# Softmax bias, rope queries and a weight fetch in another order, the last half tile cut 384 + 128: one layer of a hybrid diffusion trunk on one Trainium2 core

## The chip, the core and the metric

The kernel runs on one core of one Trainium2 chip. Its five engines are named as in the profile: PE is TensorE (matmul), DVE is VectorE, ACT is ScalarE, POOL is GpSimd and SP is SyncE, which here only issues DMAs. The metric is the device time of one execution in microseconds (us). Before the change the median of three runs is 616.72 us (616.5 to 617.53).

## The reference

One layer of a hybrid trunk for 1024 latent tokens and 128 context tokens, width 1024, float32. Each token goes through an RMSNorm with modulation and one input projection to 2496 columns, which feeds a gated MLP (group A) and a latent attention with 4 heads (group B). Latent tokens read 1024 latent keys, whose rope part is rotated, and 256 cached context keys, whose rope part isn't. Both groups' outputs go through one output projection, are gated, added to the residual, and a last RMSNorm scales each row.

```python
h = _rmsnorm(x, norm_g) * (1 + scale) + shift
u, v, g_a, c_q, c_kv, k_rope, g_b = _split_in(h @ w_in)
a_out = _chunk_mlp(u, v, w_s, b_s, g_v) * jax.nn.silu(g_a)
q = (_rmsnorm(c_q, q_norm_g) @ w_uq).reshape(B, L, MLA_HEADS, QK_NOPE + QK_ROPE)
...
attn = _block_attention(qn, (qr_rot, qr), ((kn, kr_rot, vv), (kn_c, kr_c, v_c)))   # softmax over 1024 + 256 keys
y = jnp.concatenate([a_out, attn * jax.nn.silu(g_b)], axis=-1) @ w_o
return _rmsnorm(x + gate * y, final_g)
```

## The kernel before

**Tiles and stages.** A row tile is 128 tokens: tiles 0 to 7 are the latent tokens, tile 8 is the context. Each operand of a product is held as a high and a low float32r part, and a product is three matmuls (high by high, high by low, low by high). The stages follow each other on PE: the input projection and the gated MLP (to about 300 us of the span), the transposes of queries and keys (to 318), the attention (318 to 530), and the output projection with the last norms (530 to the end).

**The attention stream.** A head is a query tile t with a head number h. `score_steps(t, h)` writes the logits of the 1024 latent keys to a PSUM tile `s1` in two halves (`lat`, lines 1515 to 1519), and those of the 256 context keys to a half of `s2` (`con`). Softmax has four steps in `softmax`: `start` (DVE maximum of the latent logits, into `m`, L1481), `shift` (DVE maximum of the context logits, L1484, and the bias `nb`, by one operation at L1489 or by two at L1486 and L1487), `exps` (ACT exponentials of the context and then the latent logits into `e`, L1495) and `divide` (DVE sum and reciprocal `rs`, L1499 and L1500, then POOL scales `e`, L1501). Two heads are a pair. `value_steps(t, pr)` then takes a pair's 1280 columns in five steps: PE transposes four 128x128 blocks of `e` into a PSUM tile `pT` (L1562), ACT copies its high part into `ph` (L1566), DVE subtracts to get the low part `pl` (L112, a helper that all such subtractions share), and PE multiplies both with the values into `o` (L1586 to L1588). After the fifth step ACT copies `o` to `os`, and PE projects it into `at` (L1605), which lies in a buffer of the same pool as `pT`; DVE multiplies it into `mixB` (L1607). So every pair of heads is one period of the stream, with one `at`.

**What sets the order.** All engines run what the program writes, in that order. A hand-kept clock `now` advances by an assumed cost with every PE step, and `later(dt, fn)` puts `fn` into the program once that clock has gone on by `dt`. So `dt` is no wait: it sets only what stands ahead of what in the queue of an engine.

**Beside the attention.** A list `units` holds 16 jobs that form sums of blocks of the output weights `w_o` for a Strassen-like output projection: SP loads `traw`, POOL forms differences, ACT copies high parts `thi`, DVE subtracts the low parts in `traw`, and SP writes all to `tdram`. They run beside query tiles 1 to 5. Later `t_pieces(m, ...)` fetches sum number m back with DMAs that POOL issues (L1919). `his` and `los` are lists of jobs for spare moments of POOL and DVE.

**Rope queries.** `q_rope_T(t)` transposes a tile's rotary queries into `qrT`, copies their high parts on ACT (L1339) and subtracts the low parts on DVE (L1347).

**Output projection and the end.** `Plan` takes steps with an engine, a cost, a priority and what they need, and writes them in the order of a greedy schedule. 28 products run with blocks of sums; five PSUM banks "w" are shared between them. `load_gate` (L2053) fetches the gate rows, with which DVE multiplies each finished product (L2194 for one of the first). `norm` ends each row tile: ACT squares, a root, three to four small DVE steps, then `y6` as one DVE operation over 128x1024 (L2120) and `y7` as two ACT operations (L2128) with DMAs from ACT's queue, after POOL multiplied with the final gain `fg` (L2132). Tile 8's right half is done early and kept; `finish_left` does its left half last: `left` writes two PSUM tiles of 256 columns (24 matmuls each, L1952 to L1954), DVE multiplies with the gate row (`zm`, L2278) and adds the residual (`za`, L2279), ACT squares, DVE forms the mean `zv` (L2286), ACT the root (L2287), four DVE steps the reciprocal root `rlast`, and DVE and ACT scale the left (L2296) and the kept right half (L2300), each with its own store.

Of the kernel before, what the change touches and what calls it, by code (L numbers as in the profile page):

```python
# [13 lines left out]
AF = mybir.ActivationFunctionType  # L14
# [6 lines left out]
NS = 8  # L21
# [73 lines left out]
def tile_hymba_step(ctx: ExitStack, tc: tile.TileContext, I, O):  # L95
# [1225 lines left out]
    def q_rope_T(t):  # L1321
# [14 lines left out]
        def part(par):  # L1336
            own = slice(64 * par, 64 * par + 64)
            oth = slice(64 - 64 * par, 128 - 64 * par)
            later(0.0, lambda: S.copy(d5[own, 2 - n :, :, par, sl], src[own]))  # L1339
# [9 lines left out]
        later(0.1 if t == 7 else 0.6, lambda: part(0))  # L1349
        later(0.15 if t == 7 else 1.2, lambda: part(1))  # L1350
# [120 lines left out]
    def softmax(t, h, lat_, con_):  # L1471
# [11 lines left out]
        def shift():  # L1483
            V.tensor_reduce(m[:, 1:2], con_, axis=AX.X, op=ALU.max)  # L1484
            if units or (t, h) == (NS - 1, 3):
                V.tensor_reduce(nb, m, axis=AX.X, op=ALU.max)  # L1486
                V.tensor_scalar(nb, nb, nscl[:, t : t + 1], None, op0=ALU.mult)  # L1487
            else:
                V.scalar_tensor_tensor(nb, m[:, 0:1], m[:, 1:2], nscl[:, t : t + 1], op0=ALU.max, op1=ALU.mult)  # L1489
            later(0.6, exps)  # L1490
            later(1.3, lambda: spare_lo(1))
# [29 lines left out]
    def score_steps(t, h):  # L1521
# [266 lines left out]
    with tc.manual_schedule(engines=engines):  # L1788
# [311 lines left out]
    def norm(g, prio):  # L2100
# [6 lines left out]
        on_v(f"n{t}v", lambda: V.tensor_scalar(fv, fs, 1.0 / 1024.0, EPS, op0=ALU.mult, op1=ALU.add), prev, prio, 0.16)  # L2107
        prev = [f"n{t}r", f"n{t}v"]
        for i, fn in enumerate((
            lambda: V.reciprocal(r(), ft),  # L2110
            lambda: V.scalar_tensor_tensor(fw, fv, -0.5, r(), op0=ALU.mult, op1=ALU.mult),
            lambda: V.tensor_tensor(fw, fw, r(), op=ALU.mult),
            lambda: V.scalar_tensor_tensor(r(), fw, 1.5, r(), op0=ALU.add, op1=ALU.mult),
# [3 lines left out]
        for i, u in enumerate(g):  # L2117
# [5 lines left out]
            if u < 7:  # L2123
                on_v(f"y{u}", scale, [*prev, "fg"], prio, 1.8 if u < 6 else 1.3)
                continue

            def scale_half(c, i=i, u=u):
                S.activation(xr[u][:, c], xr[u][:, c], AF.Copy, scale=ssq[g][:, i : i + 1])  # L2128
                nc.scalar.dma_start(O["y"][u][:, c], xr[u][:, c])

            for j, c in enumerate((R, L)):
                on_g(f"fg7.{j}", lambda c=c, u=u: G.tensor_tensor(xr[u][:, c], xr[u][:, c], fg[:, c], op=ALU.mult), [f"sq7.{j}", "fg"], 3)  # L2132
                on_s(f"y7.{j}", lambda c=c: scale_half(c), [*prev, f"fg7.{j}"], 2, 0.72)
# [125 lines left out]
    def finish_left():  # L2259
        v, v0, root, u = (small(1) for _ in range(4))  # L2260
# [6 lines left out]
        H = slice(0, 256)  # L2267

        def left(j, c):
# [3 lines left out]
            out_terms(8, cell[j][:, H], c.start, c.stop, range(8))  # L2273

        for j, c in enumerate((slice(0, 256), slice(256, 512))):
            o = lambda j=j: cell[j][:, H]
            on_t(f"pz{j}", 2.9, lambda j=j, c=c: left(j, c), [], takes=("w",) if j else ("w", "w"))
            on_v(f"zm{j}", lambda o=o, c=c: V.tensor_tensor(o(), o(), g()[:, c], op=ALU.mult), [f"pz{j}", "own0"], 0.5, 0.42)  # L2278
            on_v(f"za{j}", lambda o=o, c=c: V.tensor_tensor(o(), o(), x()[:, c], op=ALU.add), [f"zm{j}"], 0.5, 0.42)  # L2279
        square(8, 0, lambda: cell["junk"][:, 0:256], L, ["za0"], 0.5, lambda: cell[0][:, H])  # L2280
# [3 lines left out]
            "zq", lambda: S.activation(cell["junk"][:, 256:512], cell[1][:, H], AF.Square, accum_out=ssq[(8,)][:, 2:3]), ["za1"], 0.4, 0.6  # L2284
        )
        on_v("zv", lambda: V.scalar_tensor_tensor(v, ssq[(8,)][:, 2:3], 1.0 / 1024.0, v0, op0=ALU.mult, op1=ALU.add), ["zq", "zv1"], 0.4, 0.2)  # L2286
        on_s("zr", lambda: S.activation(root, v, AF.Sqrt), ["zv"], 0.3, 0.25)  # L2287
# [3 lines left out]
        on_v("zr3", lambda: V.scalar_tensor_tensor(r, u, 1.5, r, op0=ALU.add, op1=ALU.mult), ["zr2"], 0.3, 0.18)  # L2291
# [11 lines left out]
        on_v("zo0", out0, ["zr3", "fg"], 0.3, 0.7)  # L2303
# [110 lines left out]
```

## Time and profile before

| | before |
|---|---|
| median of the runs | 616.72 us |
| the profiled execution's own time | 616.81 us |
| its span on the core | 615.0 us |
| mean granted TensorE clock | 0.993 |
| PE busy | 597.7 us, 3671 instructions |
| DVE busy | 426.2 us, 932 instructions |
| ACT busy | 330.0 us, 765 instructions |
| POOL busy | 204.7 us, 243 instructions |
| bytes moved by DMA | 67.33 MB |

The span is the profiled part of an execution; 1.8 us lie around it. A row of the timeline reads: start, duration, engine, line, operation, output and inputs by the program's names (numbers of buffers left out), shape and count, and in brackets the idle time of the engine just ahead of it with what ended that time. "PE L1562" is line 1562 of the kernel before. Starts of neighbours overlap by up to some 0.1 us, since an engine begins one instruction while the one ahead of it drains.

### The profile page before, as it was taken

The page shows a single profiled execution, that of the slowest core. Times are in us where ns is not written, and L with a number is a line of the kernel's source. Part 1 is how long each engine was busy: PE and PEld are TensorE (multiplying, and loading weights), DVE is VectorE, ACT ScalarE, POOL GpSimd, SP SyncE. Part 2 cuts the span into 40 slices and gives each one's busy share as a digit, 9 for nine tenths or more (in the row PEclk, how much of TensorE's full clock was granted, in tenths as well). Part 3 has the DMA queues.
Part 4 walks back from the last instruction along what each step waited for, and adds up shares of the span by engine and source line. Part 5 has one row for each costly group of instructions (what it writes and reads, how often), then busy time and mean ns, then how long its engine had stood idle before and what let it go on. Part 6 is the DMA issues. An engine that isn't in the chain of part 4 may idle for free.

```text
span 615.0 us, 10220 instructions
## 1 busy us (share of the span) xinstructions
PE 597.7 (97%) x3671; PEld 540.0 (88%) x3671; DVE 426.2 (69%) x932; ACT 330.0 (54%) x765; POOL 204.7 (33%) x243
## 2 busy tenths in 40 slices
PE   7999999999999999999999999999999999999994
PEld 6678889999989999999998899899999988788884
DVE  3674458997746368476678677777778765478885
ACT  5656764345433345455576566566655552457543
POOL 2452112000000000443273344544444456259831
PEclk9999999999999999999999999999999999999998
DMA  8993010000351124100001033443241015961452
GB/s 316 376 371 108 0 35 2 35 0 4 135 207 70 68 84 144 41 1 1 1 14 63 1 120 129 130 138 121 95 153 46 1 70 185 388 248 44 150 174 113
DMA packets 30627, 67.33 MB, mean 109 GB/s; under 512 B 3296, under 2 KB 17392, under 8 KB 29424
## 3 DMA queue, kind: packets, MB, share of 16 engines
q1 hardware_dynamic: 27360, 55.41, 25.7%
q0 software_dynamic: 2064, 8.39, 4.0%
q10 hardware_dynamic: 1152, 2.88, 1.2%
q8 instruction: 29, 0.48, 0.3%
q14 instruction: 22, 0.18, 0.1%
HBM read 53.45 MB, written 13.21 MB: 108 GB/s over the span
## 4 chain that ended last, share of the span: by engine, by line
PE 81%; DVE 10%; ACT 4%; issue 2%; DMA 1%; SPq 0%; ACTq 0%; DVEq 0%
PE p L954 10%; PE tp L752 8%; PE tp L976 5%; PE pT L1562 4%; DVE pl L112 3%; PE zacc L1390 2%; PE zacc L1389 2%; PE zacc L1391 2%; PE S L1923 2%; DVE m L1481 2%; PE S L1924 2%; PE S L1925 2%; ACT e L1495 2%; PE s L1518 2%; PE s L1516 2%
## 5 line engine op out<-in xcount | busy, mean ns | idle before, releaser
L1501 POOL TENSOR_SCALAR e<-e,rs 128x1280 f32<-128x1280 f32 x32 | 47.1, 1472 | 101.8 <-ACT ph L1566 69.8
L1495 ACT ACTIVATE e<-s,nb,scl 128x256 f32<-128x256 f32 x64 | 56.1, 881 | 41.7 <-DVE nb L1487 21.5
L112 DVE TENSOR_TENSOR pl<-pT,ph 128x512 fp32r<-128x512 f32 x81 | 55.4, 687 | 32.5 <-ACT ph L1566 30.7
L1566 ACT CAST ph<-pT 128x512 fp32r<-128x512 f32 x80 | 46.4, 588 | 33.4 <-PE pT L1562 31.8
L1237 POOL TENSOR_TENSOR kr<-z,rope 128x64 f32<-128x64 f32 x8 | 2.6, 325 | 172.0 <-ACT z L1246 172.0
L752 PE MATMUL tp<-area,w 128*128 128x384 f32 x288 | 52.5, 338 | 0.0
L1562 PE MATMUL pT<-ident,e 128*128 128x128 f32 x320 | 48.4, 274 | 2.7 <-DVE pl L112 2.0
L752 PEld LDWEIGHTS tp<-area,w 128*128 128x128 f32 x288 | 50.4, 188 | 0.4
L1586 PE MATMUL o<-ph,vh 128*128 128x256 f32 x160 | 47.7, 298 | 0.0
L1588 PE MATMUL o<-ph,vl 128*128 128x256 f32 x160 | 45.0, 281 | 0.0
L1587 PE MATMUL o<-pl,vh 128*128 128x256 f32 x160 | 44.9, 281 | 0.0
L1562 PEld LDWEIGHTS pT<-ident,e 128*128 128x128 f32 x320 | 37.0, 140 | 7.5 <-PE at L1605 2.5
L1481 DVE TENSOR_REDUCE m<-s 128x1 f32<-128x1024 f32 x32 | 38.9, 1216 | 1.5 <-PE s L1519 1.5
L1515 PE MATMUL s<-kch,area 128*128 128x512 f32 (+2 forms) x100 | 39.1, 391 | 0.0
L1516 PE MATMUL s<-kcl,area 128*128 128x512 f32 (+2 forms) x100 | 35.3, 353 | 0.0
L1518 PE MATMUL s<-krh,area 128*128 128x512 f32 (+2 forms) x100 | 35.3, 353 | 0.0
L1519 PE MATMUL s<-krl,area 128*128 128x512 f32 (+2 forms) x100 | 35.1, 351 | 0.0
L1517 PE MATMUL s<-kch,area 128*128 128x512 f32 (+2 forms) x100 | 35.1, 351 | 0.0
L976 PE MATMUL tp<-area,w 128*128 128x384 f32 x192 | 35.0, 337 | 0.0
L976 PEld LDWEIGHTS tp<-area,w 128*128 128x128 f32 x192 | 33.6, 188 | 0.4 <-issue 0.4
L1587 PEld LDWEIGHTS o<-pl,vh 128*128 128x128 f32 x160 | 30.2, 189 | 1.4
L1586 PEld LDWEIGHTS o<-ph,vh 128*128 128x128 f32 x160 | 30.1, 188 | 1.4
(665 smaller groups left out, 1718.6 us busy)
## 6 DMA issues: line engine op xcount, KB each, us to landing
ada<-in_ada_ss SPq DMA_DIRECT2D x16, 512.0 KB, 8.7
w2r<-in_w_t SPq DMA_DIRECT2D x12, 512.0 KB, 4.3
x<-in_x SPq DMA_DIRECT2D x9, 512.0 KB, 8.2
adag<-in_ada_g SPq DMA_DIRECT2D x4, 1024.0 KB, 4.9
traw<-in_w_o SPq DMA_DIRECT2D x16, 256.0 KB, 3.4
tdram<-thi SPq DMA_DIRECT2D x32, 128.0 KB, 1.8
tdram<-traw SPq DMA_DIRECT2D x32, 128.0 KB, 1.8
wor<-in_w_o SPq DMA_DIRECT2D x8, 512.0 KB, 3.6
```

The costliest lines, as they stand in the source:

```text
L112: V.tensor_tensor(lo, src, f32(hi), op=ALU.subtract)
L752: T.matmul(tps[i, g][:, :GW], w_[i][:, k, :], x_[k, g], start=k == 0 and j == 0, stop=k == NK - 1 and j == 2)
L954: T.matmul(banks[key], a_, b_, start=k == 0 and m == 0, stop=k == 3 and m == len(passes) - 1)
L976: T.matmul(tps[c, 2][:, :GW], w_[c][:, k, :], x_[k, 2], start=k == 0 and m == 0, stop=k == NK - 1 and m == 2)
L1481: V.tensor_reduce(m[:, 0:1], lat_, axis=AX.X, op=ALU.max)
L1495: S.activation(e[:, sl], src, AF.Exp, bias=nb, scale=scl[:, t : t + 1], accum_out=su[:, i : i + 1])
L1501: G.tensor_scalar(e, e, rs, 0.0, op0=ALU.mult, op1=ALU.add)
L1516: T.matmul(ps, qh_, kcl[:, sl], start=False, stop=False)
L1518: T.matmul(ps, qr_, krh[:, sl], start=False, stop=False)
L1562: T.transpose(ps[:, w : w + P], es[t, h][:, c * P : (c + 1) * P], ident)
L1586: T.matmul(o, vh[:, kt, :], ph[:, sl], start=c == 0, stop=False)
L1587: T.matmul(o, vh[:, kt, :], pl[:, sl], start=False, stop=False)
```

## The change

Seven edits, in the order of the program. (1) The bias `nb` is formed by two DVE operations also for query tiles 0 and 1. (2) `shift` is put into the queue 0.95 after the context logits where it was 0.7, while `units` has jobs and for tile 1. (3) The rope queries of tile 7: the ACT copies are written 8.2 later on the clock of the program, where it was 0.1, and the DVE subtractions follow at 1.4 and 2.5 behind them. (4) The fetch of the third sum of weights, two DMAs of POOL's queue, is put into the program 0.6 after the fourth `plain` step instead of at the end of the list `his`. (5) In `norm` the mean is multiplied by −0.5 when it is formed; tile 7 (a norm of one column, w == 1) needs one DVE step less. (6) `y6` is done as a POOL multiplication and an ACT scaling for each half; `y7`'s halves are scaled on POOL where ACT did it; all four are stored from SP's queue. (7) The last half tile is cut into 384 and 128 columns; its rows are multiplied with `fg` ahead of the root (`zf0`, `zf1`), and the −0.5 is applied beside the root (`zw`), so that behind the root there are three small steps and one 128x512 multiplication on DVE.

```diff
@@ q_rope_T
-                later((2.2, 5.8)[par], lambda: low(own, oth))
+                later((1.4, 2.5)[par], lambda: low(own, oth))
...
-        later(0.1 if t == 7 else 0.6, lambda: part(0))
-        later(0.15 if t == 7 else 1.2, lambda: part(1))
+        later(8.2 if t == 7 else 0.6, lambda: part(0))
+        later(8.25 if t == 7 else 1.2, lambda: part(1))
@@ softmax, shift
-            if units or (t, h) == (NS - 1, 3):
+            if units or t < 2 or (t, h) == (NS - 1, 3):
@@ score_steps, con
-            later(0.7, cell["shift"])
+            later(0.95 if units or t == 1 else 0.7, cell["shift"])
@@ plain
-                his.extend([lambda n=n: t_pieces(3, 2 * n, whole[n][:, 0:4096], 1024) for n in range(2)])
+                later(0.6, lambda: [t_pieces(3, 2 * n, whole[n][:, 0:4096], 1024) for n in range(2)])
@@ norm
-        on_v(f"n{t}v", lambda: V.tensor_scalar(fv, fs, 1.0 / 1024.0, EPS, op0=ALU.mult, op1=ALU.add), prev, prio, 0.16)
+        on_v(f"n{t}v", lambda: V.tensor_scalar(fv, fs, -0.5 / 1024.0, -0.5 * EPS, op0=ALU.mult, op1=ALU.add), prev, prio, 0.16)
+        if w == 1:
+            root = [lambda: V.scalar_tensor_tensor(fw, r(), r(), fv, op0=ALU.mult, op1=ALU.mult)]
+        else:
+            root = [lambda: V.tensor_tensor(fw, fv, r(), op=ALU.mult), lambda: V.tensor_tensor(fw, fw, r(), op=ALU.mult)]
...
-                S.activation(xr[u][:, c], xr[u][:, c], AF.Copy, scale=ssq[g][:, i : i + 1])
-                nc.scalar.dma_start(O["y"][u][:, c], xr[u][:, c])
+                if u == 6:
+                    S.activation(xr[u][:, c], xr[u][:, c], AF.Copy, scale=ssq[g][:, i : i + 1])
+                else:
+                    G.tensor_scalar(xr[u][:, c], xr[u][:, c], ssq[g][:, i : i + 1], 0.0, op0=ALU.mult, op1=ALU.add)
+                nc.sync.dma_start(O["y"][u][:, c], xr[u][:, c])
@@ finish_left
+        cut_at = 384
+        own_of = (slice(0, cut_at), slice(cut_at, 512))
+        at_ = (slice(0, cut_at), slice(0, 512 - cut_at))
...
+        for j, dep in ((0, ["za1"]), (1, ["zv"])):
+            on_v(f"zf{j}", lambda j=j: V.tensor_tensor(x()[:, own_of[j]], cell[j][:, at_[j]], fg[:, own_of[j]], op=ALU.mult), [*dep, "sq8.0", "zq", "fg"] if j else [*dep, "sq8.0", "fg"], 0.6, (0.57, 0.3)[j])
...
-        on_v("zr0", lambda: V.reciprocal(r, root), ["zr"], 0.3, 0.18)
-        on_v("zr1", lambda: V.scalar_tensor_tensor(u, v, -0.5, r, op0=ALU.mult, op1=ALU.mult), ["zr0"], 0.3, 0.18)
-        on_v("zr2", lambda: V.tensor_tensor(u, u, r, op=ALU.mult), ["zr1"], 0.3, 0.18)
+        on_v("zw", lambda: V.tensor_scalar(vn, v, -0.5, None, op0=ALU.mult), ["zv"], 0.3, 0.16)
+        on_v("zr0", lambda: V.reciprocal(r, root), ["zr"], 0.2, 0.18)
+        on_v("zr2", lambda: V.scalar_tensor_tensor(u, r, r, vn, op0=ALU.mult, op1=ALU.mult), ["zr0", "zw"], 0.3, 0.18)
...
-            for j in range(2):
-                c = slice(256 * j, 256 * j + 256)
-                V.scalar_tensor_tensor(x()[:, c], cell[j][:, H], r, fg[:, c], op0=ALU.mult, op1=ALU.mult)
+            V.tensor_scalar(x(), x(), r, None, op0=ALU.mult)
             nc.sync.dma_start(O["y"][8][:, L], x())
```

Three places show what this does to the queues. The first is DVE in the attention stream, where `units` runs: the first head of a pair, here tile 3, head 2 (`m32`, `nb32`, `rs32`), beside the value steps of tile 2's second pair (`pl21_2` is its third step, `at20` the projected output of tile 2's first pair). Before:

```order
L1481 TENSOR_REDUCE m32_4410<-s132_4365 128x1
L1484 TENSOR_REDUCE m32_4410<-s2_3422 128x1
L1486 TENSOR_REDUCE nb32_4411<-m32_4410 128x1
L1487 TENSOR_SCALAR nb32_4411<-nb32_4411,nscl_94 128x1
L112 TENSOR_TENSOR pl21_2_4442<-pT21_2_4436,ph21_2_4441 128x512
L1607 TENSOR_TENSOR mixB_2045<-mixB_2045,at20_4468 128x2x128
L1499 TENSOR_TENSOR rs32_4413<-su32_4412 128x1
```

And after, at the same place:

```order
L1481 TENSOR_REDUCE m32_4416<-s132_4367 128x1
L112 TENSOR_TENSOR pl21_2_4448<-pT21_2_4442,ph21_2_4447 128x512
L1484 TENSOR_REDUCE m32_4416<-s2_3422 128x1
L1486 TENSOR_REDUCE nb32_4417<-m32_4416 128x1
L1487 TENSOR_SCALAR nb32_4417<-nb32_4417,nscl_94 128x1
L1607 TENSOR_TENSOR mixB_2045<-mixB_2045,at20_4474 128x2x128
L1499 TENSOR_TENSOR rs32_4419<-su32_4418 128x1
```

One `pl` moved from behind the bias to ahead of the context maximum. The same swap stands in eight heads, one in every pair from tile 1, head 2, to tile 5, head 0; the other head of each pair has its rows in the order of before.

The second place is POOL's queue at the end of the attention (`area0`, `area1` receive the third sum, `t1` the first; `kch5`, `krh6` and `area2` from `wor` are high parts of rows of `w_o`). Before:

```order
L115 TENSOR_SCALAR ringC_5828<-mixB_2045 128x512
L115 TENSOR_SCALAR kch5_5778<-wor5_5780 128x512 x2
L115 TENSOR_SCALAR krh6_5782<-wor6_5784 128x512 x2
L115 TENSOR_SCALAR area2_120<-wor7_5786 128x512 x2
L1919 DMA area0_118<-tdram_92 128x4x512
L1919 DMA area1_119<-tdram_92 128x4x512
L1919 DMA t1_6051<-tdram_92 128x2048 x2
```

And after:

```order
L115 TENSOR_SCALAR ringC_5834<-mixB_2045 128x512
L115 TENSOR_SCALAR kch5_5784<-wor5_5786 128x512
L1919 DMA area0_118<-tdram_92 128x4x512
L1919 DMA area1_119<-tdram_92 128x4x512
L115 TENSOR_SCALAR kch5_5784<-wor5_5786 128x512
L115 TENSOR_SCALAR krh6_5788<-wor6_5790 128x512 x2
L115 TENSOR_SCALAR area2_120<-wor7_5792 128x512 x2
L1919 DMA t1_6057<-tdram_92 128x2048 x2
```

The two DMAs of the third sum went ahead of five copies.

The third place is DVE at the end (`left0`, `left1` are the two pieces of the last half tile, `own0` its gate row and residual, `fss7` and `fss8` the row sums of tiles 7 and 8). Before:

```order
L2278 TENSOR_TENSOR left1_6694<-left1_6694,own0_6612 128x256
L2111 SCALAR_TENSOR_TENSOR smalls_6056<-smalls_6056,fss7_6682 128x1
L2279 TENSOR_TENSOR left1_6694<-left1_6694,own0_6612 128x256
L2112 TENSOR_TENSOR smalls_6056<-smalls_6056,fss7_6682 128x1
L2098 TENSOR_TENSOR smalls_6056<-smalls_6056,fss8_6188 128x1
L2113 SCALAR_TENSOR_TENSOR fss7_6682<-smalls_6056,fss7_6682 128x1
L2282 TENSOR_SCALAR smalls_6056<-smalls_6056 128x1
L2286 SCALAR_TENSOR_TENSOR smalls_6056<-fss8_6188,smalls_6056 128x1
```

And after:

```order
L2284 TENSOR_TENSOR left1_6709<-left1_6709,own0_6619 128x128
L2114 SCALAR_TENSOR_TENSOR fss7_6689<-smalls_6062,fss7_6689 128x1
L2285 TENSOR_TENSOR left1_6709<-left1_6709,own0_6619 128x128
L2293 TENSOR_TENSOR own0_6619<-left0_6661,fg_6061 128x384
L2098 TENSOR_TENSOR smalls_6062<-smalls_6062,fss8_6194 128x1
L2288 TENSOR_SCALAR smalls_6062<-smalls_6062 128x1
L2294 SCALAR_TENSOR_TENSOR smalls_6062<-fss8_6194,smalls_6062 128x1
```

The multiplication of the 384 columns with `fg` (L2293) now stands ahead of the sum over tile 8's squares (L2098), and tile 7's reciprocal root (L2114, last step) stands right behind the multiplication of the last piece.

More of the change, by code (lines that the diff above doesn't have):

```diff
@@ L2121, in scale @@
                 nc.sync.dma_start(O["y"][u], xr[u])
[L2123 to L2124 removed]
+            if u < 6:
+                on_v(f"y{u}", scale, [*prev, "fg"], prio, 1.8)
                 continue
             def scale_half(c, i=i, u=u):
[L2128 to L2133 removed]
+                if u == 6:
[3 more added lines that the diff above has]
+                nc.sync.dma_start(O["y"][u][:, c], xr[u][:, c])
+            for j, c in enumerate((L, R) if u == 6 else (R, L)):
+                on_g(f"fg{u}.{j}", lambda c=c, u=u: G.tensor_tensor(xr[u][:, c], xr[u][:, c], fg[:, c], op=ALU.mult), [f"sq{u}.{j}", "fg"], 3 + 0.1 * j)
+                (on_s if u == 6 else on_g)(f"y{u}.{j}", lambda c=c, scale_half=scale_half: scale_half(c), [*prev, f"fg{u}.{j}"], 2, 0.72)
     def name_of(q):
@@ L2259, in finish_left @@
     def finish_left():
-        v, v0, root, u = (small(1) for _ in range(4))
+        v, v0, root, u, vn = (small(1) for _ in range(5))
         r = sm.tile([P, 1], F32, tag="fr", name="rlast")
@@ L2265, in finish_left, with left @@
         on_g("z4", lambda: G.tensor_tensor(keep, keep, fg[:, R], op=ALU.mult), ["sq8.1", "fg"], 2.5)
-        H = slice(0, 256)
-        def left(j, c):
+        cut_at = 384
+        own_of = (slice(0, cut_at), slice(cut_at, 512))
+        at_ = (slice(0, cut_at), slice(0, 512 - cut_at))
+        def left(j):
             cell[j] = psw.tile([P, 512], F32, tag="w", name=f"left{j}")
@@ L2272, in left @@
                 cell["junk"] = psw.tile([P, 512], F32, tag="w", name="junk")
[L2273 to L2280, printed above, removed]
+            out_terms(8, cell[j][:, at_[j]], own_of[j].start, own_of[j].stop, range(8))
+        for j in range(2):
+            o = lambda j=j: cell[j][:, at_[j]]
+            dur = (0.57, 0.3)[j]
+            on_t(f"pz{j}", (4.3, 1.6)[j], lambda j=j: left(j), [], takes=("w",) if j else ("w", "w"))
+            on_v(f"zm{j}", lambda o=o, c=own_of[j]: V.tensor_tensor(o(), o(), g()[:, c], op=ALU.mult), [f"pz{j}", "own0"], 0.5, dur)
+            on_v(f"za{j}", lambda o=o, c=own_of[j]: V.tensor_tensor(o(), o(), x()[:, c], op=ALU.add), [f"zm{j}"], 0.5, dur)
+        square(8, 0, lambda: cell["junk"][:, own_of[0]], L, ["za0"], 0.5, lambda: cell[0][:, own_of[0]])
         sums((8,), v0, 0.5)
```

9 lines of the change are left out of this document (3 added, 6 removed).

## The prediction, made before the changed kernel was run

> **What bounds the kernel now.** I read the page first, then the timeline of PE, DVE and ACT through one pair of heads, then the places at which PE waits, then the end. The page says that PE is busy nearly all the time:
>
> ```profile
> span 615.0 us, 10220 instructions
> PE 597.7 (97%) x3671; PEld 540.0 (88%) x3671; DVE 426.2 (69%) x932; ACT 330.0 (54%) x765; POOL 204.7 (33%) x243
> ```
>
> 17.3 us of the span are not PE's, and 8.4 of them lie behind its last matmul (a row below). So an edit pays only where PE waits or behind PE's end, and it costs where it makes PE wait anew. In the attention beside `units`, PE's rows look full, but one place per pair is slower than it need be. First the projection of a pair's output and the next transposes, then the same projection 86.41 us later, then the last one of the attention, behind which an unhindered matmul follows:
>
> ```profile
> 361.94 0.60 PE L1605 MATMUL at<-os,wuv 128*128 128x128 f32 x4
> 362.70 0.63 PE L1562 MATMUL pT<-ident,e 128*128 128x128 f32 x4 [0.17 <-DVE pl L112]
> ...
> 448.35 0.60 PE L1605 MATMUL at<-os,wuv 128*128 128x128 f32 x4
> ...
> 508.34 0.60 PE L1605 MATMUL at<-os,wuv 128*128 128x128 f32 x4
> 508.70 0.47 PE L1923 MATMUL f<-area 128*128 128x512 f32 x1
> ```
>
> Four transposes behind `at` start 0.76 us after it where 0.36 is possible: 0.40 lost, waiting for a `pl` that DVE has not made. Seven pairs lie between the first two `at`, so a pair takes 12.34 us. Who sets that? DVE over the same pair:
>
> ```profile
> 359.98 1.21 DVE L1481 TENSOR_REDUCE m<-s 128x1 f32<-128x1024 f32 x1
> 361.11 0.41 DVE L1484 TENSOR_REDUCE m<-s 128x1 f32<-128x256 f32 x1
> ...
> 361.75 0.22 DVE L1487 TENSOR_SCALAR nb<-nb,nscl 128x1 f32<-128x1 f32 x1
> 361.88 0.68 DVE L112 TENSOR_TENSOR pl<-pT,ph 128x512 fp32r<-128x512 f32 x1
> ...
> 364.35 0.69 DVE L112 TENSOR_TENSOR pl<-pT,ph 128x512 fp32r<-128x512 f32 x1
> 364.96 1.22 DVE L1481 TENSOR_REDUCE m<-s 128x1 f32<-128x1024 f32 x1
> 366.36 0.69 DVE L112 TENSOR_TENSOR pl<-pT,ph 128x512 fp32r<-128x512 f32 x1 [0.19 <-ACT ph L1566]
> ...
> 370.24 0.69 DVE L112 TENSOR_TENSOR pl<-pT,ph 128x512 fp32r<-128x512 f32 x1 [1.79 <-ACT ph L1566]
> ...
> 372.33 1.22 DVE L1481 TENSOR_REDUCE m<-s 128x1 f32<-128x1024 f32 x1
> ```
>
> And ACT:
>
> ```profile
> 362.00 0.56 ACT L1495 ACTIVATE e<-s,nb,scl 128x256 f32<-128x256 f32 x1 [1.69 <-DVE nb L1487]
> ...
> 363.74 0.58 ACT L1566 CAST ph<-pT 128x512 fp32r<-128x512 f32 x1
> ...
> 369.63 0.58 ACT L1566 CAST ph<-pT 128x512 fp32r<-128x512 f32 x1
> ```
>
> Read as a ring: DVE's maximum and bias end at 361.97, ACT's exponentials start at 362.00 (it waited 1.69 for them), behind them on ACT stands `ph` at 363.74, for `ph` waits DVE's `pl` at 364.35, and behind this `pl` stands the next head's maximum at 364.96. The second head goes the same way: bias, exponentials, `ph` 369.63, `pl` 370.24 (DVE waited 1.79 for it), four more DVE steps, maximum 372.33. No link has slack: DVE and ACT hand the work to each other, and PE, with its 0.40 of waiting, follows them. The first half of the ring takes 364.96 − 359.98 = 4.98, the second 372.33 − 364.96 = 7.37, together 12.35.
>
> **The swap in the stream (edit 2).** In the first head of a pair one `pl` now stands between the two maxima. From the context maximum on, all of the first half comes later by one `pl`, whose place in the queue is 364.96 − 364.35 = 0.61: 5.59 instead of 4.98. What stands behind the bias in place of that `pl` gains nothing, since DVE then waits for ACT's exponentials in any case. In the second half something is given back: PE is no longer late, so the 0.19 of waiting ahead of the `pl` at 366.36 goes. From the maximum to that `pl` there are 366.36 − 364.96 = 1.40, and unhindered, as between the rows 359.98 and 361.11, 1.13: 0.27 less, so 7.10. The pair becomes 12.69, 0.34 more. PE's old wait behind `at` goes, since that `pl` is now early; what is late next is the `ph` and `pl` behind the exponentials, so that the transposes two steps on wait for a buffer, by 0.40 + 0.34 = 0.74 in each pair. Over seven full pairs +2.4 us. From above, a whole `pl` a pair would be 0.61 × 7 = 4.3, but the rows leave only what is not given back, and I bound it at 2.5; from below, a ring that hides all but 0.27 gives 1.9.
>
> **The start of the attention (edits 1 and 3).** Here POOL and DVE meet:
>
> ```profile
> 330.76 1.34 POOL L1501 TENSOR_SCALAR e<-e,rs 128x1280 f32<-128x1280 f32 x1 [2.36 <-DVE rs L1500]
> 330.95 1.16 DVE L1489 SCALAR_TENSOR_TENSOR nb<-m,nscl 128x1 f32<-128x1 f32 x1
> 320.76 1.18 ACT L1339 CAST area<-qrT 64x512 fp32r<-64x512 f32 x2 [0.71 <-PE qrT L1330]
> 325.99 0.66 PE L1722 MATMUL pT<-ident,e 128*128 128x128 f32 x4 [0.63 <-POOL e L1715]
> 341.01 0.63 PE L1562 MATMUL pT<-ident,e 128*128 128x128 f32 x4 [0.95 <-DVE pl L112]
> ```
>
> The one-step bias reads two operands from SBUF and ends with POOL's row (332.11 and 332.10): 1.16 us for one column, where the second step of the two-step form takes 0.22 (the row at 361.75). Edit 1 takes this out, edit 3 takes 1.18 us of ACT copies out of the way of tile 8's exponentials, for whose `e` PE waits 0.63. Gain: no more than the two waits of PE, 0.63 + 0.95 = 1.6. But behind the second wait stands ACT: with the bias on time and `shift` 0.25 later on the program's clock, the exponentials of tile 1's second head come just ahead of the `ph` of the next pair's first transposes. Then a wait for `pl` opens there, which I estimate at 1.5: the 0.95 and the 0.56 of one exponential step (the row at 362.00) that now stands in front. So the sum lies between −1.6 (nothing new) and +0.5 (only the new wait for the old, 1.5 − 0.95); I take the middle, −0.5, since the first gain and the loss rest on rows of the same kind. The copies and subtractions of edit 3 run later beside the stream's own ACT and DVE work; at worst their 1.18 us of ACT delays a `ph` there, which those ends hold.
>
> **The fetch of the third sum (edit 4).** PE's longest wait of the output projection:
>
> ```profile
> 520.07 1.57 POOL L1919 DMA_DIRECT2D area<-tdram  x2
> 527.44 0.33 SPq L2053 DMA_DIRECT2D gate<-gdram  x1
> 536.59 0.69 DVE L2194 TENSOR_TENSOR mixB<-f,gate 128x512 f32<-128x512 f32 x1 [3.70 <-DMA gate<-gdram]
> 537.38 0.47 PE L1923 MATMUL S<-t,ringC 128*128 128x512 f32 x1 [1.34 <-ACT raw L2147]
> ```
>
> DVE waits 3.70 us for the gate rows, and only when its multiplication has freed a bank "w" can PE's product at 537.38 start: 1.34 lost. The gate is asked for at 527.44, behind the fetches of POOL's queue. The third sum goes a few POOL copies earlier, but then the first sum's fetch, of the same size, comes earlier too and stands in its place. I take −0.2; if the gate's way is free it is all of −1.3. The copies that POOL now does behind two issues (1.57 us together) feed products later than these, so I cost them at nothing; if they were late, PE would wait for at most those 1.6. The Trainium skill (DMA: Bandwidth & Descriptors, "Queues, rings and completion order") says that a DMA engine takes turns between the queues that have work, packet by packet. By that rule the gate would get its turns whatever POOL's queue holds, and this term would be 0.0.
>
> **The norms (edits 5, 6).** The scaling of −0.5 moves within steps that stay; tile 6's 128x1024 operation leaves DVE (it waited for nobody there: the last piece's products end later), POOL takes four more half-tile operations. Nothing on the path but `y7`, next.
>
> **The end (edit 7).** The rows of the last half tile, and the nearest ones for its new widths:
>
> ```profile
> 151.63 4.36 PE L954 MATMUL p<-area,w 128*128 128x384 f32 x24
> 318.76 0.28 PE L1518 MATMUL s<-krh,area 128*128 128x128 f32 x1
> 319.99 0.28 PE L1519 MATMUL s<-krl,area 128*128 128x128 f32 x1
> 600.69 0.28 PE L1952 MATMUL left<-area 128*128 128x256 f32 x1
> 606.33 0.28 PE L1954 MATMUL left<-area,ml 128*128 128x256 f32 x1
> 606.66 0.42 DVE L2278 TENSOR_TENSOR left<-left,own 128x256 f32<-128x256 f32 x1
> 608.33 0.17 DVE L2286 SCALAR_TENSOR_TENSOR smalls<-fss,smalls 128x1 f32<-128x1 f32 x1
> 608.11 0.72 ACT L2128 ACTIVATE xr<-xr,fss 128x512 f32<-128x512 f32 x1
> 609.26 0.16 ACT L2287 ACTIVATE smalls<-smalls 128x1 f32<-128x1 f32 x1 [0.43 <-ACT xr L2128]
> 610.46 0.72 ACT L2300 ACTIVATE wuv<-wuv,rlast 128x512 f32<-128x512 f32 x1 [0.43 <-DVE rlast L2291]
> 611.22 0.34 ACTq L2301 DMA_DIRECT2D out_y<-wuv  x1
> L115 POOL TENSOR_SCALAR area<-mixA 128x512 fp32r<-128x512 f32 x2 | 1.2, 621 | 0.0
> ```
>
> 47 intervals of 256 columns take 606.33 − 600.69 = 5.64, so 0.120 each, 48 of them 5.76. 24 matmuls of 384 columns take 4.36 with the last one's drain of 0.28, so 4.2; 128 columns cost 1.23 / 11 = 0.112 each in the rows from 318.76 to 319.99 (eleven intervals), 24 of them 2.7. Together 6.9: PE ends 1.1 later, at 607.7. The Trainium skill (TensorE: Matmul & The Clock Gate, "Back-to-back issue gap") gives 81 ns a matmul for streams with 128 columns, from which I estimate 1.9 for these 24, and the end 0.7 earlier. The row, with this kernel's own type, decides: 2.7.
>
> Then by the queue of DVE: the last piece's first step starts at 607.7, and it holds half the columns of the row at 606.66, so some 0.2; tile 7's last root step ends at 608.1, so POOL scales `y7` from about 608.15 to 609.4 (two halves of 0.62). DVE goes on with the residual (0.2) and the 384 columns (some 0.55), and at about 608.9 comes tile 8's sum, a step with two operands in SBUF. If it is held until POOL ends, as the bias at 330.95 was, it runs at 609.4, and the mean ends at about 610.05; else it ends at 609.5. Before, it ended at 608.50, but ACT was held up by `y7` (608.11, then the next step at 609.26), so the root is later by 0.8, or 0.3. From the root to ACT's last scaling there were 610.46 − 609.26 = 1.2; one step of 0.2 is gone and ACT waits behind no DMA issue of its own for `y7` (0.2 of its idle 0.43): 0.8. So ACT's store starts at 611.6 against 611.22: +0.4, and at 611.1 (−0.1) if nothing is held. I take +0.4, since the nearest row is held in just this way; from −0.3 to +1.0 with half a microsecond either way.
>
> **The sum.** 616.81 − 0.5 + 2.4 − 0.2 + 0.4 = 618.9, less the 0.09 by which the profiled execution is above the median: 618.8 us. About 0.2%, 1.2 us, is what a measurement of this kernel can tell from no change, so 615.5 to 617.9 counts as the same.
>
> **Rivals.** (a) The ring has slack that its rows don't show, and the swap frees PE: then the 0.40 behind `at` goes in seven pairs, −2.8 in place of +2.4, and the time is 613.6. This decides if the exponentials can start later without the next maximum starting later. For it speaks that PE's only wait in each pair is for that `pl`; against it that ACT waits 1.69 and DVE 1.79 for each other and both waits end on the other's last step. Chance 0.10. (b) The gate lands early and PE's 1.34 goes: 617.7, about the same as before; for it speaks that the fetch is asked for 9.2 us before its use, against it that the first sum's bytes are still ahead. Chance 0.20. (c) The swap hands its loss back in the second half, +2.4 becomes 0: 616.4. Chance 0.05; the second half has only 0.19 of waiting to give. My forecast has 0.65.
>
> The range takes in the bounds of the terms above (616.81 + 0.0 for the start + 2.5 − 0.2 + 1.0 − 0.09 = 620.0), and below 616.8, to which case (b) reaches with a start that gains 0.9 more; the cases (a) and (c) are left out. Faster by over 0.2% is (a), 0.10; the same is (b) and (c), 0.25; slower is the forecast, 0.65.
>
> **What would show it.** In the profile after: the `at` rows (L1605 before) some 12.7 apart through the seven pairs, a `pl` between the two maxima, no wait behind `at`, and instead about 0.7 of waiting for `pl` at the third transposes of a pair. One-column bias steps of 0.2 at 330. PE's wait for the product behind the gate still above 1 us. PE's last matmul some 7 us after the first of the last half tile, tile 8's sum ending together with POOL's second half of `y7`, and ACT's last store issued 3.9 us behind PE's end. I am wrong if the pairs take 12.3 or less, if the gate's wait is gone, or if the last store follows PE's end by less than 3.4.

## The result and the profile after

The changed kernel takes 617.95 us (median, 617.24 to 619.39, 16 runs), the kernel before 616.86 us (615.78 to 618.52, 16 runs). The ratio is 1.0017 with a 95% interval of 1.0008 to 1.0026: slower by 1.1 us, between 0.5 and 1.6. So the sign is clear of the noise, but the size, 0.17%, lies inside the band of 0.2% that the prediction had called "the same", and to which it gave 0.25. The predicted 618.8 us is 0.85 above the median, and the median lies within the stated range of 616.8 to 620.0.

The top of the page of the kernel after; PE is busy 1.7 us longer, of which 1.1 are the dearer last piece:

```profile
span 615.5 us, 10221 instructions
PE 599.4 (97%) x3671; PEld 541.4 (88%) x3671; DVE 425.4 (69%) x936; ACT 328.9 (53%) x765; POOL 207.4 (34%) x247
```

PE's timeline of the kernel after, one pair in the stretch with `units` and the first and tenth `at` (line numbers behind the first 2000 lines are moved by a few; L1605 is the same line):

```profile
349.08 0.60 PE L1605 MATMUL at<-os,wuv 128*128 128x128 f32 x4
...
411.56 0.61 PE L1605 MATMUL at<-os,wuv 128*128 128x128 f32 x4
412.00 0.60 PE L1562 MATMUL pT<-ident,e 128*128 128x128 f32 x4
...
421.25 0.66 PE L1562 MATMUL pT<-ident,e 128*128 128x128 f32 x4 [0.43 <-DVE pl L112]
...
424.20 0.60 PE L1605 MATMUL at<-os,wuv 128*128 128x128 f32 x4
...
461.80 0.60 PE L1605 MATMUL at<-os,wuv 128*128 128x128 f32 x4
```

The transposes behind `at` now follow after 0.44 (0.76 before): the wait there is gone. In its place PE waits 0.43 for a `pl` at the third transposes of the next pair, and the pair takes 424.20 − 411.56 = 12.64 us instead of 12.34. DVE in the same pair, and ACT's first exponentials of its two heads:

```profile
409.96 1.22 DVE L1481 TENSOR_REDUCE m<-s 128x1 f32<-128x1024 f32 x1
411.09 0.68 DVE L112 TENSOR_TENSOR pl<-pT,ph 128x512 fp32r<-128x512 f32 x1
411.69 0.42 DVE L1484 TENSOR_REDUCE m<-s 128x1 f32<-128x256 f32 x1
...
415.53 1.22 DVE L1481 TENSOR_REDUCE m<-s 128x1 f32<-128x1024 f32 x1
416.66 0.68 DVE L112 TENSOR_TENSOR pl<-pT,ph 128x512 fp32r<-128x512 f32 x1
...
422.58 1.22 DVE L1481 TENSOR_REDUCE m<-s 128x1 f32<-128x1024 f32 x1
```

```profile
412.57 0.56 ACT L1495 ACTIVATE e<-s,nb,scl 128x256 f32<-128x256 f32 x1 [2.61 <-DVE nb L1487]
...
418.15 0.56 ACT L1495 ACTIVATE e<-s,nb,scl 128x256 f32<-128x256 f32 x1 [2.04 <-DVE nb L1487]
```

The `pl` stands between the two maxima, the context maximum begins 1.73 behind the first one (1.13 before), and ACT waits 2.61 for the bias where it waited 1.69. The halves of the ring are 415.53 − 409.96 = 5.57 and 422.58 − 415.53 = 7.05.

Where the time lies can be told stage by stage, since every profile passes the same marks: a query product (L158) that closes the input stage, the first and the tenth `at`, PE's product behind the gate rows, the first matmul of the last half tile, the issue of ACT's last store, and the end of the span. In us from mark to mark:

| | before | after | without edit 2 | edit 2 alone | unit jobs moved | all gains |
|---|---|---|---|---|---|---|
| start of the span to the query product | 304.88 | 304.56 | 306.45 | 304.01 | 305.68 | 304.83 |
| to the first `at` | 45.07 | 44.52 | 43.72 | 45.00 | 43.76 | 43.75 |
| to the tenth `at` | 110.38 | 112.72 | 110.76 | 112.35 | 107.87 | 107.88 |
| to the product behind the gate rows | 77.05 | 76.25 | 76.38 | 76.69 | 76.32 | 76.50 |
| to the last half tile | 63.31 | 63.32 | 63.31 | 63.33 | 63.32 | 63.31 |
| to the issue of the last store | 10.53 | 10.54 | 10.54 | 10.51 | 10.54 | 9.58 |
| to the end of the span | 3.78 | 3.59 | 3.54 | 3.81 | 3.51 | 3.55 |

The last four columns are experiments, below. The first row is a stage that no kernel here changes, and in 13 profiles it lies between 304.01 and 307.23, as wide as the times of one kernel scatter. It goes with the TensorE clock that was granted in the first 25 us: 304.01 to 304.83 in the three profiles with 1.00 there, 304.56 to 305.68 in five with 0.93, 305.34 to 307.23 in five with 0.86. The other rows repeat within 0.1 us in kernels that have the same edits there (within 0.6 on the way to the product behind the gate rows), so the stages are compared by them. From before to after: start −0.55, attention beside `units` +2.34, fetch and gate −0.80, end 0.0 and −0.2. There are nine pairs from the first to the tenth `at`; seven of them took 12.31 to 12.37 before, the first and the last 11.99 and 11.98.

### The profile page after: what moved, and what is told of

Read it like the earlier page. It is cut to its first block, busy times and chain, and to the rows that moved or that the text cites. A ratio compares the mean times of both kernels' runs of the same rounds, so it can differ in the third digit from the quotient of the medians.

```text
span 615.5 us, 10221 instructions
## 1 busy us (share of the span) xinstructions
PE 599.4 (97%) x3671; PEld 541.4 (88%) x3671; DVE 425.4 (69%) x936; ACT 328.9 (53%) x765; POOL 207.4 (34%) x247
## 4 chain that ended last, share of the span: by engine, by line
PE 70%; DVE 16%; ACT 8%; issue 4%; DMA 1%; SPq 0%; ACTq 0%; DVEq 0%
PE p L954 10%; PE tp L752 8%; DVE pl L112 6%; PE tp L976 5%; ACT e L1495 5%; DVE m L1481 4%; PE zacc L1390 2%; PE zacc L1389 2%; PE zacc L1391 2%; PE S L1923 2%; PE S L1924 2%; PE S L1925 2%; ACT ph L1566 2%; DVE m L1484 2%; PE A L1924 1%
```

## The experiments

**Without edit 2.** The changed kernel with one line as before:

```diff
-            later(0.95 if units or t == 1 else 0.7, cell["shift"])
+            later(0.7, cell["shift"])
```

> The changed kernel with edit 2 alone undone: the bias step is again put into the queue 0.7 after the context logits everywhere. Theory (the ring of DVE and ACT sets the pair): the pairs beside `units` take 12.35 us again, with 0.4 of waiting behind each `at` and no wait at the third transposes; 2.3 us less than the changed kernel, about 615.6 us, faster than the kernel before by the gains of the start, the fetch and the end (0.5 + 0.7 + 0.1). Rival (the longer pairs come from something else that changed, such as the two-step bias or the DMAs): the pairs stay near 12.6 and the time stays at 617.9.

Measured: 615.33 us (614.01 to 617.65, 11 runs), ratio to the kernel before 0.9966 (0.9952 to 0.9981): 2.1 us faster than before. The long pairs are back at 12.34 to 12.37 (one takes 12.69). So one line makes the whole loss, and the rest of the change is a gain. The first `at` comes 1.35 earlier than before, 0.8 earlier than in the changed kernel, which had not been expected: edit 2 costs at the start too.

**Edit 2 alone.** The same line in the kernel before.

> The kernel before with edit 2 alone (0.95 in place of 0.7 while `units` has jobs and for tile 1). Theory of the ring: pairs of 12.65, +2.3 over eight heads, and up to +0.5 at the start, where the exponentials of tile 1 come later: 619.2 to 619.7 us, slower than the whole change. Rival (PE's wait behind `at` was what cost, and the swap takes it away): 2.8 less, 614.

Measured: 619.09 us (617.46 to 619.67, 11 runs), ratio 1.0028 (1.0016 to 1.0039), +1.0 to +2.4 us. The nine pairs take 1.97 more than before, with PE's waits of 0.43 for `pl` where the changed kernel has them. The rival that had PE freed is out. The start is not later (45.00), so there the 0.95 costs only what edits 1 and 3 would gain.

**Edit 4 alone** (the earlier fetch of the third sum).

> The kernel before with edit 4 alone (the third sum's fetch goes out earlier). Theory: the gate rows land some 8.4 us behind their request instead of 9.15, since less stands in front of them in the DMA engines, and PE's wait of 1.34 ahead of the product behind the gate shrinks by 0.7: 616.1 us. Rival (the gate landed earlier in the changed kernel only because the longer attention gave the DMAs 1.4 us more): the wait stays at 1.3, 616.9 us.

Measured: 617.23 us (615.90 to 618.25, 11 runs), ratio 0.9999 (0.9986 to 1.0011). The first row below is PE's product behind the gate in this kernel, the others are from edit 2 alone and from edit 1 alone, neither of which has edit 4:

```profile
537.75 0.47 PE L1923 MATMUL S<-t,ringC 128*128 128x512 f32 x1 [0.63 <-ACT ringB L2149]
```

```profile
538.05 0.48 PE L1923 MATMUL S<-t,ringC 128*128 128x512 f32 x1 [0.54 <-ACT ringB L2149]
```

```profile
537.00 0.48 PE L1923 MATMUL S<-t,ringC 128*128 128x512 f32 x1 [1.08 <-ACT raw L2147]
```

The wait is 0.63 with the edit alone. Over all profiles it is 0.53 to 1.34 in the six kernels without the edit, and 0.57 to 0.96 in the seven with it. In all 13 profiles the wait is 7.81 to 7.84 less than the time from the gate rows' request to their first use, so PE does wait for the gate. But that time, 8.35 to 9.15 without the edit and 8.41 to 8.80 with it, doesn't follow the edit. So the 1.34 of the one profile before was the top of a scatter, and neither theory held: there was no wait of 1.3 for this edit to win. From the tenth `at` to that product, six kernels without the edit take 76.73 in the mean (76.44 to 77.05), seven with it 76.42 (76.25 to 76.76): some 0.3, part of it short waits of 0.2 to 0.4 for a low part of `w_o` that four of the six show between 517 and 522 us and none of the seven. The timing can't tell 0.3 from nothing.

**Edits 5 to 7 alone** (norms, tiles 6 and 7, the cut at 384).

> The kernel before with edits 5 to 7 alone (norms, scaling of tiles 6 and 7, the cut at 384). Theory from the two traces: PE ends 1.1 later, and behind it 1.1 to 1.3 less is needed, so nothing moves: 616.7 to 616.9 us. Rival (the prediction's): tile 8's sum held by POOL's scaling, +0.4: 617.3 us; then that sum's row would be longer than 0.4 us.

Measured: 616.41 us (615.73 to 618.84, 12 runs), ratio 0.9996 (0.9982 to 1.0011): nothing. From the first matmul of the last half tile to the last store 10.56 us, before 10.53.

**Edit 1 alone and edit 3 alone** (the bias in two steps; the rope queries later).

> The kernel before with edit 1 alone (the bias of tiles 0 and 1 in two DVE steps). The first experiment put the gain of edits 1 and 3 together at 1.35 us, read where the first pair's output is projected. Theory: PE's two waits at the start have one cause each, the held bias for the wait of 0.95 ahead of the transposes of tile 0, the ACT copies for the wait of 0.63 ahead of tile 8's. Then edit 1 alone gains about 0.9, the first `at` stands 44.2 behind the first query rope product instead of 45.07, and the bias rows take 0.2: 616.0 us. Rival (one edit does it all): 0 or 1.35.

> The kernel before with edit 3 alone (rope queries of tile 7 later). Theory of one cause each: the wait of 0.63 ahead of tile 8's transposes goes, the one of 0.95 stays, the first `at` at 44.5 instead of 45.07: 616.3 us. Rival: the copies now stand in front of exponentials of tile 0, and nothing or less is gained: 616.9 us.

Measured: 616.52 us, ratio 1.0002 (0.9990 to 1.0014), and 616.63 us, ratio 1.0005 (0.9991 to 1.0018). The marks say more: the first `at` at 44.44 with edit 1 and at 45.35 with edit 3 (before 45.07). PE's wait in this stretch, with edit 1:

```profile
326.36 0.66 PE L1722 MATMUL pT<-ident,e 128*128 128x128 f32 x4 [0.66 <-POOL e L1715]
```

and with edit 3:

```profile
336.90 0.63 PE L1562 MATMUL pT<-ident,e 128*128 128x128 f32 x4 [0.72 <-DVE pl L112]
341.00 0.63 PE L1562 MATMUL pT<-ident,e 128*128 128x128 f32 x4 [1.01 <-DVE pl L112]
```

where DVE has

```profile
329.83 1.15 DVE L1489 SCALAR_TENSOR_TENSOR nb<-m,nscl 128x1 f32<-128x1 f32 x1
331.02 1.39 DVE L1347 TENSOR_TENSOR area<-qrT,area 64x512 fp32r<-64x512 f32 x2
...
335.01 1.15 DVE L1489 SCALAR_TENSOR_TENSOR nb<-m,nscl 128x1 f32<-128x1 f32 x1
336.08 1.27 DVE L112 TENSOR_TENSOR pl<-pT,ph 128x512 fp32r<-128x512 f32 x2
```

Edit 1 takes the wait of 0.95 away and leaves tile 8's. Edit 3 takes tile 8's away, but then PE waits 0.72 for the `pl` at 336.08, and nothing is won. DVE has no pause between the first and the last of these rows: two held biases (1.15 each) and the moved rope subtractions (1.39) stand in it. With edit 1 as well, the subtractions are there too and PE doesn't wait, so it is the held bias that costs; which of the two was not separated. Together the edits gain 1.35, more than −0.63 and +0.28 make: edit 3 pays only once edit 1 is there. "One cause each" was right for edit 1 and wrong for edit 3.

**The 0.95 for `units` alone.** The changed kernel with

```diff
-            later(0.95 if units or t == 1 else 0.7, cell["shift"])
+            later(0.95 if units else 0.7, cell["shift"])
```

> The changed kernel with the 0.95 only while `units` has jobs, 0.7 again for the heads of tile 1 before that. Theory: the part of edit 2 for tile 1 is what takes 0.8 us of the start's gain back, the part for `units` is what makes the pairs longer. Then the first `at` stands 43.7 behind the first query rope product (44.52 in the changed kernel), without PE's wait of 1.19 ahead of the second pair's transposes, and the pairs still take 12.6: 617.2 us. Rival (the late start of those heads only hides what the longer pairs would cost anyway): the first `at` is earlier, but the end is not: 617.9 us.

Measured: 617.52 us (616.17 to 619.28, 12 runs), ratio 1.0015 (1.0004 to 1.0026). The first `at` is at 43.73, without the wait of 1.19, and the nine pairs take 112.70, as in the changed kernel: by the marks the theory. The time alone (1.0015 against 1.0017) can't show the 0.8.

**The unit jobs out of the ring.** Without edit 2, and with the second high and low part of each unit job moved:

```diff
-            for dt, fn, i in ((3.2, high, 0), (4.6, low, 0), (5.0, high, 1), (6.4, low, 1)):
+            for dt, fn, i in ((3.2, high, 0), (4.6, low, 0), (3.25, high, 1), (4.65, low, 1)):
```

> The changed kernel without edit 2, and in each unit job the second high part is put 3.25 behind the start instead of 5.0, and the second low part 4.65 instead of 6.4, so that both run while DVE and ACT wait for each other instead of between a `pl` and the next maximum. Theory of the ring: 0.6 us of DVE leave the second half of the ring, so PE becomes the bound: the wait of 0.4 behind each `at` goes, the pairs take 11.95, and seven to eight pairs give 2.8 to 3.2: 612.4 us. Rival (PE's own order or the buffers of the transposes set the pair): the pairs stay at 12.35, 615.3 us.

Measured: 612.63 us (611.53 to 614.04, 6 runs), ratio 0.9938 (0.9923 to 0.9953). If a ring of DVE and ACT sets the pair, then any DVE step taken out of it must shorten the pair until PE is full, and this does. The busy time from 350 to 450 us, by engine (PE first; then PE's weight loads, DVE, ACT, POOL), in the changed kernel:

```profile
350.00:450.00 100.00, 97.30 (x670) 88.30 (x668) 71.86 (x159) 60.41 (x128) 45.49 (x46) 1.00 0.37 119
```

without edit 2:

```profile
350.00:450.00 100.00, 98.62 (x683) 90.11 (x682) 73.98 (x159) 62.55 (x130) 45.57 (x46) 1.00 0.37 122
```

and with the unit jobs moved:

```profile
350.00:450.00 100.00, 100.00 (x704) 92.50 (x703) 76.43 (x164) 64.26 (x132) 45.63 (x49) 1.00 0.40 127
```

PE's 2.70, 1.38 and 0.0 of idle time are what the ring left. DVE is busier each time, with the same work in less time. In the last kernel the two low parts stand together where DVE waits for ACT anyway:

```profile
391.04 1.29 DVE L112 TENSOR_TENSOR traw<-traw,thi 128x512 fp32r<-128x512 f32 x2
393.33 0.69 DVE L112 TENSOR_TENSOR pl<-pT,ph 128x512 fp32r<-128x512 f32 x1 [1.00 <-ACT ph L1566]
```

and DVE still waits 1.00 behind them. The pairs take 11.98 or 11.99. The edit moves an ACT copy (`thi`, 0.63) along with each subtraction. In the kernel before, the second `pl` of such a place starts 1.48 behind the first, though its `ph` is ready after 0.98; with the jobs moved it starts after 0.88. So by the rows 0.5 of the 0.6 are the subtraction's, but the two were not moved one at a time.

**The same move in the kernel before, alone.**

> The kernel before with the move of the second high and low part of each unit job alone. Theory of the ring: the pairs take 11.97 instead of 12.34, eight of them, 2.9 less than the kernel before: 614.0 us, with no wait behind `at`. Rival (the gain hung on the earlier start of edits 1 and 3): less than 1.5 us.

Measured: 614.17 us (614.01 to 614.95, 6 runs), ratio 0.9964 (0.9952 to 0.9977). Pairs of 11.98, nine in 107.88 instead of 110.38: 2.5 us, a little less than the 2.9 expected, since seven pairs were long and not eight (7 × 0.36). It doesn't need the earlier start.

**The cut at 256.** Without edit 2, and

```diff
-        cut_at = 384
+        cut_at = 256
```

with the planner's costs of the pieces as before.

> The changed kernel without edit 2, and with the last half tile cut at 256 again, the rest of edit 7 kept. Theory: the cut at 384 made PE end 1.1 us later, and the steps ahead of the root took 1.1 less, so that edit 7 gained nothing; with the cut at 256 PE ends 1.1 earlier, and the last piece's DVE and ACT steps, 128 columns wider, give back about 0.4. So 0.7 less than without edit 2: 614.6 us, the last store issued 9.9 behind the first matmul of the half tile instead of 10.54. Rival (behind PE's end the POOL scaling of `y7` is late next, or the chain of tile 7): no gain, 615.3 us.

Measured: 614.85 us (613.05 to 616.19, 12 runs), ratio 0.9965 (0.9952 to 0.9978). The last store is issued 9.57 behind the first matmul of the half tile (10.54 with the cut at 384):

```profile
606.34 0.28 PE L1954 MATMUL left<-area,ml 128*128 128x256 f32 x1
```

```profile
610.28 0.35 ACTq L2307 DMA_DIRECT2D out_y<-wuv  x1
```

So the rest of edits 5 to 7 is worth 1.0 us up to the last store, and the cut at 384 costs all of it. In the times against the kernel before the 1.0 doesn't show apart from the scatter (0.9965 and 0.9966, each against its own runs of the kernel before).

**All gains.** Edits 1 and 3 to 7 without edit 2, cut at 256, unit jobs moved.

> Edits 1, 3, 4, 5, 6 and 7 without edit 2, with the cut at 256 and the move of the unit jobs. Theory: the gains lie in different stages and add up: start 1.35, pairs 2.9 to 3.1, end 0.9: 611.7 us. Rival (the gate rows, asked for 8.4 us before they land, become the bound when the attention ends earlier): PE's wait ahead of the product behind the gate grows by as much as is saved, and the time stays at 612.6 us.

Measured: 611.62 us (610.94 to 613.29, 6 runs), ratio 0.9925 (0.9909 to 0.9941): 4.6 us faster than the kernel before. The marks add up (the table's last column), and PE's wait behind the gate stays at 0.81.

## Why the prediction was right, and where its sizes were off

**The ring** was read right. Its halves were forecast at 5.59 and 7.10 and measured at 5.57 and 7.05, and the new wait opened at the third transposes. PE's row shows 0.43 of it where 0.74 was forecast; against the 11.98 of a pair in which PE never waits, a pair of 12.64 loses 0.66. +2.4 was forecast and +2.34 is what the marks show, but the closeness is luck: edit 2 alone makes +1.97, and undoing it in the changed kernel takes 1.96 away; the other 0.35 is one slow pair that is there without edit 2 as well (12.69 in the first experiment, 12.95 in the changed kernel), in the kernels that have edit 1. Nor are the 1.97 seven pairs of 0.34: five pairs take 12.6 or more, some 0.3 longer than before; at the edges the steps differ (12.29 for the second pair, 12.47 and 12.52 for the eighth and ninth), and the ninth, 11.98 before and not among the seven, adds 0.5. The lower bound of 1.9 had no row behind it: 0.27 a pair is what the second half hands back, not what it leaves. That the ring sets the pair is shown from both sides: a step put into it costs, a step taken out gains until PE is full. Rival (a), slack in the ring, and rival (c), the loss handed back, are refuted: in the second half the way from the maximum to the next `pl` shrank from 1.40 to 1.13, and these 0.27 were all that it had to give.

**The start** came out at the −0.5 that was taken (−0.55), and by its mechanism: both waits went, and a new one of 1.19 for `pl` opened where 1.5 was estimated:

```profile
342.71 0.63 PE L1562 MATMUL pT<-ident,e 128*128 128x128 f32 x4 [1.19 <-DVE pl L112]
```

The prediction named edit 2's part in it; that this part costs 0.8, and that edits 1 and 3 are worth 1.35 without it, only the experiments showed.

**The fetch** was taken at −0.2. In the profiles it is −0.80, by the means of six and seven kernels −0.3, by the time nothing that can be told. In the kernel after, PE's wait is 0.57, where the prediction had it stay above 1; the 0.77 less are nearly all of the −0.80:

```profile
538.05 0.47 PE L1923 MATMUL S<-t,ringC 128*128 128x512 f32 x1 [0.57 <-ACT ringB L2152]
```

The step that was weak is the one that took 1.34, a wait seen in one profile, as the size of the thing. Rival (b) had no 1.3 to win. The gate rows start to be used 8.44 us behind their request with edit 4 alone and 8.38 with edit 2 alone, which is what the rule of taking turns, that the prediction cited from the Trainium skill (DMA: Bandwidth & Descriptors, "Queues, rings and completion order"), would give; that the queues took turns is not shown by it.

**The end** was taken at +0.4 and is 0.0 at the store, −0.2 at the end of the span. PE did end 1.1 later:

```profile
601.37 0.33 PE L1952 MATMUL left<-area 128*128 128x384 f32 x1
608.07 0.28 PE L1954 MATMUL left<-area,ml 128*128 128x128 f32 x1
```

Between the first and the last matmul lie 6.70, where 5.64 lay before. A matmul of 128 columns takes 0.112, so it was right to let the row decide. The 81 ns of the Trainium skill (TensorE: Matmul & The Clock Gate, "Back-to-back issue gap") do not fit this stream. The step that failed is "if it is held until POOL ends, as the bias at 330.95 was". POOL, DVE and ACT at the end of the kernel after:

```profile
608.92 1.36 POOL L2131 TENSOR_SCALAR xr<-xr,fss 128x512 f32<-128x512 f32 x2 [3.06 <-DVE fss L2114]
```

```profile
609.39 0.15 DVE L2098 TENSOR_TENSOR smalls<-smalls,fss 128x1 f32<-128x1 f32 x1
...
609.86 0.16 DVE L2294 SCALAR_TENSOR_TENSOR smalls<-fss,smalls 128x1 f32<-128x1 f32 x1
610.24 0.17 DVE L2296 TENSOR_SCALAR smalls<-smalls 128x1 f32<-128x1 f32 x1 [0.22 <-ACT smalls L2295]
610.32 0.28 DVE L2293 TENSOR_TENSOR own<-left,fg 128x128 f32<-128x128 f32 x1
610.51 0.16 DVE L2297 RECIPROCAL rlast<-smalls 128x1 f32<-128x1 f32 x1
```

```profile
610.05 0.16 ACT L2295 ACTIVATE smalls<-smalls 128x1 f32<-128x1 f32 x1 [0.64 <-DVE smalls L2294]
611.16 0.72 ACT L2306 ACTIVATE wuv<-wuv,rlast 128x512 f32<-128x512 f32 x1 [0.95 <-DVE rlast L2299]
```

The sum ran in 0.15 with POOL at work. The bias was the wrong row to go by: the prediction took the sum for "a step with two operands in SBUF", but of the inputs of the sum and of the mean only `fss` lies there; `smalls` is a PSUM tile in the code. What that makes is in the last section. A smaller error went the other way: behind the root the −0.5 step and the last 128 columns (610.24 and 610.32) stand ahead of the reciprocal, so the way from root to ACT's scaling is 1.11, not the 0.8 that was reckoned (1.20 before). ACT's store is issued 3.56 behind PE's end, between the forecast 3.9 and the 3.4 that was to prove it wrong.

**The sum.** −0.55, +2.34, −0.3 to −0.8 and −0.2 make +0.8 to +1.3 where +2.1 was forecast; the median moved by 1.1. Both misses, the end and the fetch, leaned the same way, and the forecast stood only 0.9 beyond the border of 617.9 to "the same". A chance of 0.65 for slower by over 0.2% left too little for that: with the lower bounds of the end and the fetch the very same ring lands inside the band. The range's upper end also took 0.0 for the start, whose own bound was +0.5.

## What to carry to other kernels

Where PE looks 99% busy and two engines hand work back and forth, write down which steps stand between one handover and the next: their sum, not PE, may be the period, and a step that has nothing to do with the handover (here the `traw` subtraction) belongs where an engine waits. A wait that disappears is no gain until it is known what set the period. And a number that rests on one profiled wait, such as the 1.34 ahead of the product behind the gate, should be taken as one draw from a scatter. Before a held step is taken as a model for another one, look where the operands of both lie.

## What the runs showed of the hardware that was not expected

The one-step bias, a DVE step on one column with all inputs in SBUF, was held to the end of POOL's scaling of 128x1280 each time it started beside one: 18 times in the six profiles that have it in tiles 0 and 1, ending within 0.01 us of POOL. It took 1.15 to 1.17 us where it started 0.19 behind POOL, and 0.54 and 0.56 where it started 0.8 behind (edit 2 alone), instead of 0.22. The width of POOL's operation doesn't decide, since in the kernel before it was also held beside one of 128x512 (496.65 and 496.64 are the ends):

```profile
495.34 1.30 POOL L806 TENSOR_TENSOR mixA<-mixA,mixB 128x512 f32<-128x512 f32 x1
```

```profile
496.25 0.40 DVE L1489 SCALAR_TENSOR_TENSOR nb<-m,nscl 128x1 f32<-128x1 f32 x1
```

The sum and the mean at the end, with one input in PSUM, ran in 0.15 and 0.16 beside POOL's 128x512. Two DVE subtractions of one shape differ in the same way in the kernel before, this time by what they do to POOL:

```profile
383.46 0.69 DVE L112 TENSOR_TENSOR traw<-traw,thi 128x512 fp32r<-128x512 f32 x1
389.03 0.69 DVE L112 TENSOR_TENSOR pl<-pT,ph 128x512 fp32r<-128x512 f32 x1
```

```profile
383.74 1.62 POOL L1501 TENSOR_SCALAR e<-e,rs 128x1280 f32<-128x1280 f32 x1 [4.11 <-ACT ph L1566]
389.11 1.35 POOL L1501 TENSOR_SCALAR e<-e,rs 128x1280 f32<-128x1280 f32 x1 [2.24 <-ACT ph L1566]
```

Beside the subtraction with both inputs in SBUF, POOL's scaling takes 1.62; beside `pl`, which reads `pT` from PSUM, 1.35. So all these rows fit one reading, that the two engines are in each other's way when DVE takes two inputs from SBUF; no run moved an operand to test it. In the rows of the start, edit 1 avoids the hold at no price that shows: two steps, begun at the same moment, are done in 0.4.

In the five kernels that have edit 1 and the unit jobs in their old place, one pair, the fourth, takes 0.3 us longer than its neighbours; in the five without edit 1 none does. That is half of the 0.63 which edit 1 alone gains at the start. Ahead of that pair, in the changed kernel as without edit 2, a `traw` subtraction starts 1.22 behind its `pl` instead of 0.88, 0.07 behind the moment at which POOL begins to scale, and POOL's scaling takes 1.89 or 1.90 instead of 1.62. The cause wasn't tried.
